# Joining the two parts of x into one product of 512 columns, and the two heads of a stick-breaking pair

## The chip, the cores and the metric

The kernel runs on one core of one Trainium2 chip. The metric is the device time of one execution in microseconds (us), taken from the first to the last instruction on the chip; lower is better. Several executions are measured and their median is compared.

## The reference, cut to what matters

A sequence of 256 tokens of width 1024 goes through two blocks, each of two layers, all in float32:

```
# first block, per layer
proj  = h @ w_in                      # 2048 columns: pool mixer, q, k, v
y_sb  = stick_breaking_attention(q, k, v)     # 8 heads of 64
h     = layer_norm(alpha*h + concat(pool_mixer(u), y_sb) @ w_out)
f     = (silu(h @ wg) * (h @ wu)) @ wd        # layer 0: one network of width 2816
                                              # layer 1: 8 experts of it, 2 per token
h     = layer_norm(alpha*h + f)
# stick-breaking attention, s < t only
A[t,s] = sigmoid(z_ts) * prod_{s<j<t} (1 - sigmoid(z_tj)),  z = q k^T / 8
# second block, per layer
z = rms_norm(x) @ w_in                # HGRN2 (q, f, i, g), 3 groups of dilated attention, 2 gates
x = x + (sigmoid(za)*(o_hg @ w_a) + sigmoid(zb)*(o_att @ w_b)) @ w_out
x = x + square(relu(rms_norm(x) @ w_up)) @ w_down      # width 4096
```

## The kernel before, in words

**Numbers in two parts.** Every large product is made of three matmuls of reduced-precision floats (fp32r). A weight tile `raw` is split into `whi` (ScalarE, L164) and `wlo` = raw - whi (VectorE, L166); activations are split into `xh` and `xl` likewise. `mm3` (L214 to L225) issues whi·xh, whi·xl and wlo·xh into the same PSUM columns.

**Weights.** `list_weights` writes out the order of all weight units, each 128 x 2048 floats (1 MB). `take` (L193) hands the next unit to the products: before it does, it emits the split of the unit two further on (`N_SPLIT` = 3, the present one counted), ScalarE first, then VectorE, and the DMA of a unit some eight ahead. Raw, whi and wlo tiles share 13 slots of the pool `wts`. The order of instructions on each engine is the order in which the program emits them; no scheduler moves them.

**Feature chunks.** `chunk_feat` (L273) makes 512 features for all 256 tokens, features on partitions: weights stationary, x moving with 256 columns. A chunk takes two weight units (j = 0, 1, the halves of the contraction); in each it goes over four blocks c of 128 features, and for each block over four contraction tiles with one `mm3` each, so 96 matmuls a chunk. The four blocks fill two PSUM banks of the pool `acc` (four banks), two blocks to a bank. There are 44 such chunks: 2 in each of the two stick-breaking mixers (q and k), 10 in the feed-forward network of layer 0 (`ffn`, L684), and in each layer of the second block (`second`, L1070) 2 for HGRN2, 6 for q and k of the dilated attention and 7 in the up part. `chunk_tok` (L252) is the sister with tokens on partitions and 512 moving columns; `down` (L290) is the product after the feed-forward or up part, with 512 moving columns.

**Side work.** Attention, pool mixing and the like are generators in the list `side`; `pump` advances the first two of them by one step. `chunk_feat` pumps after its second and fourth block, four times a chunk. Side work uses the PSUM pools `ms` and `tr` (two banks each). `down` drains what is left.

**What follows a chunk.** In `ffn` (L700 to L706): one Silu over the two gate blocks (ScalarE), one product with the two up blocks (VectorE), the high part (ScalarE), the low part (VectorE), all 512 wide. In the up part (L1171 to L1177), twice a chunk: Relu (ScalarE), product (VectorE), high part (ScalarE), low part (VectorE), 512 wide. For q and k of the dilated attention (L1118): two copies by ScalarE. The first chunk of both parts comes from `boundary` with tokens on partitions; the generator `first` evaluates it in one step and, in the next, transposes it into `tr` banks and splits it.

**Stick pair.** `stick_pair` (L606) is the side work for two heads, one after the other, each in a bank of its own (`ms`, then `tr`): scores, then Relu, VectorE, Exp, Ln, VectorE, then, two pumps later, the suffix sums by matmul and the last Exp. A pair takes five steps.

Of the kernel before, what the change touches and what calls it, by code (L numbers as in the profile page):

```python
# [10 lines left out]
F32 = mybir.dt.float32  # L11
F32R = mybir.dt.float32r
# [9 lines left out]
P = 128  # L22
T = 256
# [72 lines left out]
class Net:  # L96
# [176 lines left out]
    def chunk_feat(self, x):  # L273

        xh, xl = x
        out = [self.bank(), self.bank()]
        for j in range(2):
            w = self.take(1)[0]
            for c in range(4):
                o = out[c // 2][:, (c % 2) * T:(c % 2 + 1) * T]  # L280
                for k in range(4):
                    kt = 4 * j + k
                    self.mm3(o, xh[:, kt, :], xl[:, kt, :], w[0][:, k, c * P:(c + 1) * P],
                             w[1][:, k, c * P:(c + 1) * P], kt == 0 and c % 2 == 0, kt == 7,
                             w_stationary=True, skip_group_check=True)
                if c % 2 == 1:
                    self.pump()
        return out
# [137 lines left out]
    def run(self, stop=None):  # L426
# [4 lines left out]
        self.x = (self.main.tile([P, KT, T], F32R, name="xh"), self.main.tile([P, KT, T], F32R, name="xl"))  # L431
# [132 lines left out]
    def mixer(self, l, ps):  # L564
# [3 lines left out]
        with self.mixs:  # L568
# [12 lines left out]
            for j in range(2):  # L581
                ps = self.chunk_feat(self.x)
                nc.scalar.activation(q[:, 2 * j:2 * j + 2].rearrange("p c t -> p (c t)"), ps[0], AF.Identity,
                                     scale=0.125)
                nc.vector.tensor_copy(k[:, 2 * j:2 * j + 2].rearrange("p c t -> p (c t)"), ps[1])
                for c in (2 * j, 2 * j + 1):
                    self.side.append(self.stick_pair(c, q, k, pairs, work))
# [18 lines left out]
    def stick_pair(self, c, q, k, pairs, work):  # L606
        nc = self.nc
        mm = nc.tensor.matmul
        pairs[c] = []
        for hp in range(2):  # L610
            rows = slice(64 * hp, 64 * hp + 64)
            z = self.tr.tile([P, 512], F32, name="tr") if hp else self.ms.tile([P, 512], F32, name="ms")
            mm(z[:, 0:256], k[rows, c, 0:P], q[rows, c, :], start=True, stop=False, skip_group_check=True)
            mm(z[:, 256:384], k[rows, c, P:T], q[rows, c, P:T], start=False, stop=False, skip_group_check=True)
            for o in (0, 256):
                mm(z[:, o:o + P], self.identb, self.below, start=False, stop=False, skip_group_check=True)
            e = work.tile([P, 384], F32, name="e")
            pos = work.tile([P, 384], F32, name="pos")
            nc.scalar.activation(pos, z[:, 0:384], AF.Relu)
            nc.vector.scalar_tensor_tensor(e, pos, -2.0, z[:, 0:384], op0=OP.mult, op1=OP.add)  # L620
            nc.scalar.activation(e, e, AF.Exp)
            nc.scalar.activation(e, e, AF.Ln, bias=1.0)
            nc.vector.tensor_add(e, e, pos)
            yield
            yield
# [10 lines left out]
            pairs[c].append(att)  # L636
# [45 lines left out]
    def ffn(self, ps):  # L682
        nc, a, tc = self.nc, self.a, self.tc
        with tc.tile_pool(name="ffn", bufs=1) as pool, tc.tile_pool(name="ffnw", bufs=2) as work:  # L684
# [13 lines left out]
            self.side.append(first())  # L698
            for j in range(1, FF // 256):
                ps2 = self.chunk_feat(self.x)  # L700
                s = work.tile([P, 512], F32, name="s")
                nc.scalar.activation(s, ps2[0], AF.Silu)
                nc.vector.tensor_mul(s, s, ps2[1])
                h, l = (m[:, 2 * j:2 * j + 2].rearrange("p c t -> p (c t)") for m in hid)
                nc.scalar.activation(h, s, AF.Identity)
                nc.vector.tensor_sub(l, s, h.bitcast(F32))  # L706
                if j == 6:
                    g, b = self.load_rows((a["ln2_g"][0], a["ln2_b"][0]))
# [133 lines left out]
    def experts(self, gate, rank, xt, rest, iota1, sums, end):  # L842
        nc, a, tc = self.nc, self.a, self.tc
        mm = nc.tensor.matmul
        with tc.tile_pool(name="moew", bufs=2) as work:
# [4 lines left out]
            def gather(p):  # L850
# [7 lines left out]
                for i in range(2):  # L858
                    for k in range(0, KT, 2):
# [8 lines left out]
                        nc.scalar.activation(xg[i][:, k:k + 2].rearrange("p k s -> p (k s)"), ps, AF.Identity)  # L868
# [202 lines left out]
    def second(self, l, ps, stop=None):  # L1071
        nc, a, tc = self.nc, self.a, self.tc
        self.n_ahead = N_AHEAD - 1
        with tc.tile_pool(name="z", bufs=1) as pool, tc.tile_pool(name="zw", bufs=2) as work:
# [12 lines left out]
            ps = self.chunk_feat(self.x)  # L1087
            for i in range(2):
                c = slice(512 * i, 512 * i + 512)
                nc.scalar.activation(f[:, c], ps[i], AF.Sigmoid)  # L1090
                nc.scalar.activation(k[:, c], ps[i], AF.Sigmoid, scale=-1.0)
            for h in range(4):
                c = slice(T * h, T * h + T)
                nc.vector.tensor_scalar(f[:, c], f[:, c], lb[:, 4 + h:5 + h], lb[:, h:h + 1], op0=OP.mult, op1=OP.add)
                nc.vector.tensor_scalar(k[:, c], k[:, c], lb[:, 4 + h:5 + h], None, op0=OP.mult)
            ps = self.chunk_feat(self.x)
            for i in range(2):
                c = slice(512 * i, 512 * i + 512)
                nc.scalar.activation(q[:, c], ps[i], AF.Sigmoid)
                nc.vector.tensor_mul(q[:, c], q[:, c], ps[i])  # L1100
            og = pool.tile([P, 2, 512], F32, name="og")
# [8 lines left out]
            for g in range(3):  # L1110
                qk = []
                for i in range(2):
                    ps = self.chunk_feat(self.x)
                    if i == 1:
                        self.rotate(*qk[0], rope)
                    x = pool.tile([P, 4, T], F32, name="qa" if i == 0 else "ka", bufs=2)
                    for j in range(2):
                        nc.scalar.activation(x[:, 2 * j:2 * j + 2].rearrange("p c t -> p (c t)"), ps[j], AF.Identity)  # L1118
# [35 lines left out]
        with tc.tile_pool(name="up", bufs=1) as pool, tc.tile_pool(name="upw", bufs=2) as work:  # L1154
# [13 lines left out]
            self.side.append(first())  # L1168
            for j in range(1, FF2 // 512):
                ps2 = self.chunk_feat(self.x)  # L1170
                for i in range(2):  # L1171
                    s = work.tile([P, 512], F32, name="s")
                    nc.scalar.activation(s, ps2[i], AF.Relu)
                    nc.vector.tensor_mul(s, s, ps2[i])
                    h, lo = (m[:, 4 * j + 2 * i:4 * j + 2 * i + 2].rearrange("p c t -> p (c t)") for m in hid)
                    nc.scalar.activation(h, s, AF.Identity)
                    nc.vector.tensor_sub(lo, s, h.bitcast(F32))  # L1177
# [218 lines left out]
```

## Time and profile before

| what | value |
|---|---|
| median of 3 runs | 2150.21 us (2146.05 to 2150.62) |
| the profiled execution's own time | 2147.67 us |
| its span, first to last instruction | 2145.9 us |
| granted TensorE clock, mean | 0.991 of full speed |
| TensorE (PE) busy | 2097.9 us, 98% |
| VectorE (DVE) busy | 1497.7 us, 70% |
| ScalarE (ACT) busy | 1217.4 us, 57% |
| HBM read | 504.77 MB |

How to read it: PE is a matmul, PEld a weight load, L12 a line of the kernel. A matmul's duration is its latency: matmuls overlap, so the distance between the starts of two neighbours, not the duration, is what one costs in a stream. Queues of ACT and DVE are worked off in order. In what follows W stands for the ScalarE instruction of L164 (the high part of a weight unit) and w for the VectorE instruction of L166 (its low part).

### The profile page before, as it was taken

How to read it: one execution, taken by the hardware profiler on the slowest of the kernel's cores; microseconds unless marked ns; L12 is line 12 of the kernel's file. 1: busy time of each engine (PE TensorE's matmuls, PEld its weight loads, DVE VectorE, ACT ScalarE, POOL GpSimd, SP SyncE). 2: the span in 40 equal slices, each digit the busy share in tenths (PEclk: the TensorE clock that was granted, in tenths of full speed). 3: DMA queues.
4: the chain of work that ended last, by engine and by line, in shares of the span. 5: the costliest groups of instructions: out<-in, count | busy, mean ns of one | idle time of the engine just before them, and what ended most of it. 6: DMA issues, size and time to landing. Idle time of an engine off the chain costs nothing. (4 is left out here: it accounts for less than half of the span.)

```text
span 2145.9 us, 28621 instructions
## 1 busy us (share of the span) xinstructions
PE 2097.9 (98%) x11787; PEld 1823.0 (85%) x11787; DVE 1497.7 (70%) x1326; ACT 1217.4 (57%) x1199; POOL 81.0 (4%) x91
## 2 busy tenths in 40 slices
PE   7999999999999999999999799999999999999998
PEld 6889988788888888888888699988998899988987
DVE  6465464698888989898989566666655566666643
ACT  4544445677777777777777444464543434454542
POOL 1000000000000000000000101100000011100000
PEclk9999999999999999999999899999999999999999
DMA  9275555599999999999998454444754654436551
GB/s 319 79 224 188 190 163 216 192 357 367 364 339 368 368 348 361 373 350 348 367 357 305 142 182 140 144 159 138 235 191 144 222 164 155 136 130 221 191 194 62
DMA packets 240122, 509.33 MB, mean 237 GB/s; under 512 B 9360, under 2 KB 56592, under 8 KB 239984
## 3 DMA queue, kind: packets, MB, share of 16 engines
q1 hardware_dynamic: 236448, 496.21, 66.7%
q0 software_dynamic: 3248, 10.69, 1.6%
q8 instruction: 95, 1.56, 0.3%
q10 hardware_dynamic: 288, 0.52, 0.1%
q14 instruction: 43, 0.35, 0.0%
HBM read 504.77 MB, written 1.05 MB: 236 GB/s over the span
## 5 line engine op out<-in xcount | busy, mean ns | idle before, releaser
L166 DVE TENSOR_TENSOR wlo<-raw,whi 128x2048 fp32r<-128x2048 f32 x463 | 1062.1, 2296 | 356.9 <-ACT whi L164 308.0
L164 ACT ACTIVATE whi<-raw 128x2048 fp32r<-128x2048 f32 x467 | 887.0, 1915 | 259.2 <-PE acc L224 81.3
L223 PE MATMUL acc<-whi,xh 128*128 128x512 f32 x1168 | 469.1, 402 | 4.1 <-ACT xh L348 2.1
L224 PE MATMUL acc<-wlo,xh 128*128 128x512 f32 x1168 | 458.3, 392 | 2.3 <-DVE wlo L161 1.7
L225 PE MATMUL acc<-whi,xl 128*128 128x512 f32 x1168 | 459.9, 394 | 0.5 <-DVE xl L349 0.5
L219 PE MATMUL acc<-xh,whi 128*128 128x256 f32 x1408 | 404.8, 287 | 0.0
L221 PE MATMUL acc<-xh,wlo 128*128 128x256 f32 x1408 | 399.1, 283 | 0.0
L220 PE MATMUL acc<-xl,whi 128*128 128x256 f32 x1408 | 399.1, 283 | 0.0
L223 PE MATMUL acc<-whi,hidh 128*128 128x512 f32 x696 | 273.0, 392 | 0.0
L224 PE MATMUL acc<-wlo,hidh 128*128 128x512 f32 x696 | 271.6, 390 | 0.0
L219 PEld LDWEIGHTS acc<-xh,whi 128*128 128x128 f32 x1408 | 270.4, 192 | 1.3
L225 PE MATMUL acc<-whi,hidl 128*128 128x512 f32 x696 | 271.4, 390 | 0.0
L220 PEld LDWEIGHTS acc<-xl,whi 128*128 128x128 f32 x1408 | 270.5, 192 | 0.7
L221 PEld LDWEIGHTS acc<-xh,wlo 128*128 128x128 f32 x1408 | 270.3, 192 | 0.0
L225 PEld LDWEIGHTS acc<-whi,xl 128*128 128x128 f32 x1168 | 220.7, 189 | 52.6 <-DVE xl L349 5.9
L223 PEld LDWEIGHTS acc<-whi,xh 128*128 128x128 f32 x1168 | 221.2, 189 | 50.5 <-ACT xh L348 5.5
L224 PEld LDWEIGHTS acc<-wlo,xh 128*128 128x128 f32 x1168 | 221.3, 190 | 46.5 <-DVE wlo L161 2.3
L225 PEld LDWEIGHTS acc<-whi,hidl 128*128 128x128 f32 x696 | 130.8, 188 | 27.4
L223 PEld LDWEIGHTS acc<-whi,hidh 128*128 128x128 f32 x696 | 130.9, 188 | 25.9
L224 PEld LDWEIGHTS acc<-wlo,hidh 128*128 128x128 f32 x696 | 130.9, 188 | 25.7
L348 ACT ACTIVATE xh<-tr 128x512 fp32r<-128x512 f32 x40 | 22.5, 596 | 73.1 <-PE tr L355 72.8
L926 ACT ACTIVATE hidh<-tr 128x512 fp32r<-128x512 f32 (+1 forms) x48 | 27.0, 563 | 64.6 <-PE tr L355 64.6
(304 smaller groups left out, 1598.2 us busy)
## 6 DMA issues: line engine op xcount, KB each, us to landing
raw<-in_moe_wd_dram SPq DMA_DIRECT2D x88, 1024.0 KB, 6.7
raw<-in_moe_wg_dram SPq DMA_DIRECT2D x80, 1024.0 KB, 6.4
raw<-in_moe_wu_dram SPq DMA_DIRECT2D x80, 1024.0 KB, 6.3
raw<-in_w_in_dram SPq DMA_DIRECT2D x74, 1024.0 KB, 5.4
raw<-in_w_up_dram SPq DMA_DIRECT2D x32, 1024.0 KB, 5.4
raw<-in_w_down_dram SPq DMA_DIRECT2D x32, 1024.0 KB, 5.0
raw<-in_w_out_dram SPq DMA_DIRECT2D x16, 1024.0 KB, 5.0
raw<-in_ffn_wg_dram SPq DMA_DIRECT2D x22, 512.0 KB, 4.1
```

The source lines that it names most:

```text
L164: self.nc.scalar.activation(hi, raw, AF.Identity)
L166: self.nc.vector.tensor_sub(lo, raw, hi.bitcast(F32))
L219: mm(out, wh, xh, start=start, stop=False, **kw)
L220: mm(out, wh, xl, start=False, stop=False, **kw)
L221: mm(out, wl, xh, start=False, stop=stop, **kw)
L223: mm(out, xh, wh, start=start, stop=False, **kw)
L224: mm(out, xh, wl, start=False, stop=False, **kw)
L225: mm(out, xl, wh, start=False, stop=stop, **kw)
L348: self.nc.scalar.activation(h, v, AF.Identity)
L926: nc.scalar.activation(h[:, :n], v, AF.Identity)
```

## The change

`xh` and `xl` become the two halves of one tile `xx` (contraction tile, part, token), so one matmul moves both: whi·(xh, xl) with 512 columns into a whole bank, then wlo·xh with 256 columns into the bank's second half. A block now needs a bank of its own, and its two halves have to be added. `chunk_feat` no longer returns banks: it calls `sink(c, halves)` as soon as block c is complete, and each sink copies the first half (ScalarE) and adds the second (VectorE). Without `pools` the four banks come from `acc`; in the feed-forward and up parts blocks 0 and 1 take `acc` banks, block 2 a `tr` bank, block 3 an `ms` bank. `first` is advanced by its first step ahead of the chunks. `stick_pair` issues the scores of both heads together, with Abs, Exp, Ln and one VectorE instruction in place of Relu, VectorE, Exp, Ln, VectorE; a pair still takes five steps.

```diff
-    def chunk_feat(self, x):
+    def chunk_feat(self, sink, pools=None):
...
             for c in range(4):
-                o = out[c // 2][:, (c % 2) * T:(c % 2 + 1) * T]
+                if j == 0:
+                    out.append((pools or (self.acc,) * 4)[c].tile([P, 512], F32, ...))
                 for k in range(4):
                     kt = 4 * j + k
-                    self.mm3(o, xh[:, kt, :], xl[:, kt, :], w[0][:, k, c * P:(c + 1) * P], ...)
+                    mm(out[c], w[0][:, k, cw], self.xx[:, kt].rearrange("p i t -> p (i t)"), start=kt == 0, ...)
+                    mm(out[c][:, T:], w[1][:, k, cw], self.xx[:, kt, 0], start=False, stop=kt == 7, ...)
+                if j == 1:
+                    sink(c, (out[c][:, :T], out[c][:, T:]))
                 if c % 2 == 1:
                     self.pump()
...
     def stick_pair(self, c, q, k, pairs, work):
+        zs = [self.ms.tile([P, 512], F32, name="ms"), self.tr.tile([P, 512], F32, name="tr")]
+        for z, rows in zip(zs, heads):
             mm(z[:, 0:256], k[rows, c, 0:P], q[rows, c, :], start=True, stop=False, skip_group_check=True)
+        for z, rows in zip(zs, heads):
             mm(z[:, 256:384], k[rows, c, P:T], q[rows, c, P:T], start=False, stop=False, skip_group_check=True)
...
+            nc.scalar.activation(e, z[:, 0:384], AF.Abs)
+            nc.scalar.activation(e, e, AF.Exp, scale=-1.0)
             nc.scalar.activation(e, e, AF.Ln, bias=1.0)
-            nc.vector.tensor_add(e, e, pos)
+            nc.vector.scalar_tensor_tensor(e, z[:, 0:384], 0.0, e, op0=OP.max, op1=OP.add)
...
     def ffn(self, ps):
-            self.side.append(first())
+            f = first()
+            next(f)
+            self.side.append(f)
             for j in range(1, FF // 256):
-                ps2 = self.chunk_feat(self.x)
...
+                def sink(c, ps, j=j, gs=gs, us=us):
+                    s = us[:, c - 2] if c > 1 else gs[:, c]
+                    nc.scalar.activation(s, ps[0], AF.Identity)
+                    nc.vector.tensor_add(s, s, ps[1])
+                    if c < 2:
+                        nc.scalar.activation(s, s, AF.Silu)
+                    else:
+                        h, l = (m[:, 2 * j + c - 2] for m in hid)
+                        nc.vector.tensor_mul(s, s, gs[:, c - 2])
+                        nc.scalar.activation(h, s, AF.Identity)
+                        nc.vector.tensor_sub(l, s, h.bitcast(F32))
+
+                self.chunk_feat(sink, (self.acc, self.acc, self.tr, self.ms))
...
     def second(self, l, ps, stop=None):
+            def joined(dst, ps):
+                nc.scalar.activation(dst, ps[0], AF.Identity)
+                nc.vector.tensor_add(dst, dst, ps[1])
...
+                    def sink(c, ps, i=i, x=x):
+                        if i == 1 and c == 3:
+                            self.rotate(*qk[0], rope)
+                        joined(x[:, c], ps)
...
             for j in range(1, FF2 // 512):
-                ps2 = self.chunk_feat(self.x)
...
+                def sink(c, ps, j=j):
+                    v = work.tile([P, T], F32, name="s2")
+                    joined(v, ps)
+                    nc.vector.scalar_tensor_tensor(v, v, 0.0, v, op0=OP.max, op1=OP.mult)
+                    h, lo = (m[:, 4 * j + c] for m in hid)
+                    nc.scalar.activation(h, v, AF.Identity)
+                    nc.vector.tensor_sub(lo, v, h.bitcast(F32))
+
+                self.chunk_feat(sink, (self.acc, self.acc, self.tr, self.ms))
```

In the two HGRN2 chunks the sink joins the halves and then applies Sigmoid (twice for the forget gate) block by block. In the mixers the sinks of q and k are one ScalarE and one VectorE instruction a block. The gather of the expert layer writes its copy of x through the strided `xx`.

## Rows read from the trace of the kernel before

**Rows 1.** The page, part 1: busy us, share and instructions.
```profile
PE 2097.9 (98%) x11787; PEld 1823.0 (85%) x11787; DVE 1497.7 (70%) x1326; ACT 1217.4 (57%) x1199; POOL 81.0 (4%) x91
```
**Rows 2.** PE's waits over the span: us in total, times, longest.
```profile
PE tr L355 <- DVE r L423: 14.0, 2, 12.1
PE tr L355 <- ACT whi L160: 11.6, 1, 11.6
```
**Rows 3.** The page, part 5: feature chunk's first matmul (busy us, mean ns).
```profile
L219 PE MATMUL acc<-xh,whi 128*128 128x256 f32 x1408 | 404.8, 287 | 0.0
```
**Rows 4.** Timeline of PE in an up chunk: start us, us; ten matmuls.
```profile
2007.81 0.28 PE L219 MATMUL acc<-xh,whi 128*128 128x256 f32 x1
...
2008.89 0.28 PE L219 MATMUL acc<-xh,whi 128*128 128x256 f32 x1
```
**Rows 5.** Timeline of PE in the down part; seven matmuls.
```profile
2079.73 0.39 PE L225 MATMUL acc<-whi,hidl 128*128 128x512 f32 x1
...
2081.09 0.39 PE L225 MATMUL acc<-whi,hidl 128*128 128x512 f32 x1
```
**Rows 6.** Busy time of one up chunk: us, PE, PEld, DVE, ACT, POOL.
```profile
2005.54:2017.06 11.52, 11.52 (x99) 11.52 (x98) 7.26 (x7) 6.17 (x6) 0.00 (x0) 1.00 0.62 187
```
**Rows 7.** Timeline of ACT in the up part.
```profile
2006.90 0.63 ACT L1176 ACTIVATE hidh<-s 128x512 fp32r<-128x512 f32 x1 [0.76 <-DVE s L1174]
2007.44 1.90 ACT L164 ACTIVATE whi<-raw 128x2048 fp32r<-128x2048 f32 x1
2011.25 1.91 ACT L164 ACTIVATE whi<-raw 128x2048 fp32r<-128x2048 f32 x1 [1.91 <-PE acc L221]
```
**Rows 8.** Timeline of DVE in the same stretch.
```profile
2007.57 0.69 DVE L1177 TENSOR_TENSOR hidl<-s,hidh 128x512 fp32r<-128x512 f32 x1 [0.70 <-ACT hidh L1176]
2009.37 2.29 DVE L166 TENSOR_TENSOR wlo<-raw,whi 128x2048 fp32r<-128x2048 f32 x1 [1.11 <-ACT whi L164]
2013.20 2.29 DVE L166 TENSOR_TENSOR wlo<-raw,whi 128x2048 fp32r<-128x2048 f32 x1 [1.53 <-ACT whi L164]
2015.41 0.68 DVE L1174 TENSOR_TENSOR s<-s,acc 128x512 f32<-128x512 f32 x1
```
**Rows 9.** Groups by form, 256 columns wide: busy us, mean ns.
```profile
L651 ACT ACTIVATE mixh<-ms 128x256 fp32r<-128x256 f32 x8 | 3.1, 384 | 9.6 <-PE ms L649 9.6
L1354 DVE TENSOR_TENSOR oa<-oa,ms 128x256 f32<-128x256 f32 x8 | 3.4, 421 | 8.4 <-PE ms L1348 8.0
L1353 DVE TENSOR_TENSOR oa<-oa,w 128x256 f32<-128x256 f32 x8 | 3.3, 414 | 0.0
```
**Rows 10.** Timeline of DVE, an instruction that reads its predecessor's result.
```profile
1317.30 0.69 DVE L1321 TENSOR_REDUCE w<-ms 128x2 f32<-128x512 f32 x1
1318.02 0.17 DVE L1322 TENSOR_SCALAR w<-w 128x2 f32<-128x2 f32 x1
```
**Rows 11.** Timeline of DVE and ACT in the feed-forward part.
```profile
155.48 2.29 DVE L166 TENSOR_TENSOR wlo<-raw,whi 128x2048 fp32r<-128x2048 f32 x1 [1.11 <-ACT whi L164]
157.81 1.92 ACT L164 ACTIVATE whi<-raw 128x2048 fp32r<-128x2048 f32 x1 [2.36 <-DVE wlo L166]
203.95 1.91 ACT L164 ACTIVATE whi<-raw 128x2048 fp32r<-128x2048 f32 x1 [2.41 <-PE acc L220]
```
**Rows 12.** Timeline: the split of `first` in the up part, ACT and DVE.
```profile
1976.31 1.08 ACT L348 ACTIVATE hidh<-tr 128x512 fp32r<-128x512 f32 x2 [5.46 <-PE tr L355]
1976.94 1.29 DVE L349 TENSOR_TENSOR hidl<-tr,hidh 128x512 fp32r<-128x512 f32 x2 [2.75 <-ACT hidh L348]
```
**Rows 13.** Timeline of PE: one head's scores in a stick pair.
```profile
359.63 0.70 PE L613 MATMUL ms<-q,k 64*128 64x256 f32 x2
360.17 0.38 PE L614 MATMUL ms<-q,k 64*128 64x128 f32 x2
```
**Rows 14.** Timeline in the dilated attention: a w, and the evictions of a q chunk.
```profile
1322.40 2.29 DVE L166 TENSOR_TENSOR wlo<-raw,whi 128x2048 fp32r<-128x2048 f32 x1 [1.29 <-ACT whi L164]
1325.99 1.08 ACT L1118 ACTIVATE qa<-acc 128x512 f32<-128x512 f32 x2
```

More of the change, by code (lines that the diff above doesn't have):

```diff
@@ L271, in chunk_tok @@
         return out
-    def chunk_feat(self, x):
-        xh, xl = x
-        out = [self.bank(), self.bank()]
+    def chunk_feat(self, sink, pools=None):
+        mm = self.nc.tensor.matmul
+        out = []
         for j in range(2):
@@ L581, in mixer @@
             for j in range(2):
[L582 to L585, printed above, removed]
+                def sink(c, ps, j=j):
+                    if c < 2:
+                        d = q[:, 2 * j + c]
+                        nc.scalar.activation(d, ps[0], AF.Identity, scale=0.125)
+                        nc.vector.scalar_tensor_tensor(d, ps[1], 0.125, d, op0=OP.mult, op1=OP.add)
+                    else:
+                        d = k[:, 2 * j + c - 2]
+                        nc.scalar.activation(d, ps[0], AF.Identity)
+                        nc.vector.tensor_add(d, d, ps[1])
+                self.chunk_feat(sink)
                 for c in (2 * j, 2 * j + 1):
@@ L608, in stick_pair @@
         mm = nc.tensor.matmul
[L609 to L612, printed above, removed]
+        heads = (slice(0, 64), slice(64, P))
+        zs = [self.ms.tile([P, 512], F32, name="ms"), self.tr.tile([P, 512], F32, name="tr")]
+        for z, rows in zip(zs, heads):
             mm(z[:, 0:256], k[rows, c, 0:P], q[rows, c, :], start=True, stop=False, skip_group_check=True)
+        for z, rows in zip(zs, heads):
             mm(z[:, 256:384], k[rows, c, P:T], q[rows, c, P:T], start=False, stop=False, skip_group_check=True)
+        for z in zs:
             for o in (0, 256):
                 mm(z[:, o:o + P], self.identb, self.below, start=False, stop=False, skip_group_check=True)
[L617 to L621, printed above, removed]
+        es = []
+        for z in zs:
+            e = work.tile([P, 384], F32, name="e", bufs=4)
+            nc.scalar.activation(e, z[:, 0:384], AF.Abs)
+            nc.scalar.activation(e, e, AF.Exp, scale=-1.0)
             nc.scalar.activation(e, e, AF.Ln, bias=1.0)
-            nc.vector.tensor_add(e, e, pos)
+            nc.vector.scalar_tensor_tensor(e, z[:, 0:384], 0.0, e, op0=OP.max, op1=OP.add)
+            es.append(e)
             yield
-            yield
+        yield
+        for hp, (z, e) in enumerate(zip(zs, es)):
             mm(z[:, 0:256], self.suffix, e[:, 0:256], start=False, stop=False, skip_group_check=True)
@@ L635, in stick_pair @@
             nc.scalar.activation(att, z[:, 0:384], AF.Exp)
-            pairs[c].append(att)
+            pairs.setdefault(c, []).append(att)
+            if hp == 0:
+                yield
     def stick_values(self, v, pairs, mix):
@@ L1112, in second @@
                 for i in range(2):
-                    ps = self.chunk_feat(self.x)
-                    if i == 1:
-                        self.rotate(*qk[0], rope)
                     x = pool.tile([P, 4, T], F32, name="qa" if i == 0 else "ka", bufs=2)
-                    for j in range(2):
-                        nc.scalar.activation(x[:, 2 * j:2 * j + 2].rearrange("p c t -> p (c t)"), ps[j], AF.Identity)
+                    def sink(c, ps, i=i, x=x):
+                        if i == 1 and c == 3:
+                            self.rotate(*qk[0], rope)
+                        joined(x[:, c], ps)
+                    self.chunk_feat(sink)
                     rot = pool.tile([32, 4, T], F32, name="rot")
@@ L1166, in first, with sink @@
                     self.split_to(hid, self.transpose4(hs[t]), 0, t)
-            self.side.append(first())
+            f = first()
+            next(f)
+            self.side.append(f)
             for j in range(1, FF2 // 512):
-                ps2 = self.chunk_feat(self.x)
[L1171 to L1177, printed above, removed]
+                def sink(c, ps, j=j):
+                    v = work.tile([P, T], F32, name="s2")
[5 more added lines that the diff above has]
+                self.chunk_feat(sink, (self.acc, self.acc, self.tr, self.ms))
             acc3 = self.down(hid, FF2 // P)
```

50 lines of the change are left out of this document (26 added, 24 removed).

## The prediction

> **What bounds the kernel now.** I read the page first: PE is busy for 98% of the span, DVE for 70% [rows 1]. A busy matmul need not be a matmul at its peak, so I went on to PE's waits: the two longest, 14.0 and 11.6 us, lie where a layer begins or the kernel starts [rows 2] and have nothing to do with the chunks. Inside the feature chunks PE waits for nobody. What one matmul costs there is read from the timeline and not from its duration of 287 ns [rows 3], which is latency: nine distances in a chunk make 1.08 us, so a matmul of 256 columns costs 120.0 ns [rows 4]; six distances of the down part make 1.36 us, so one of 512 columns costs 226.7 ns [rows 5]. The difference, 106.7 ns for 256 columns, leaves 13.3 ns that every matmul costs whatever its width. A chunk of 96 matmuls takes 11.52 us of PE, and in that time DVE is busy for 7.26 and ACT for 6.17 us [rows 6]. So the bound is the number and width of the matmuls, and two helpers stand behind it with some room.
>
> **What the joint product gives.** Three matmuls of 256 columns (360.0 ns) become one of 512 and one of 256: 226.7 + 120.0 = 346.7 ns. The weights are loaded behind the neighbouring matmul in both streams [rows 4, 5], so I take the loads as hidden in the mixture too. A chunk falls from 11.52 to 11.09 us; 44 chunks with 32 such groups save 1408 x 13.3 ns = 18.7 us: 1.7 in the mixers, 4.3 in the feed-forward part, 6.8 in HGRN2 and attention, 6.0 in the up parts. The bounds are 18.7 us and nothing.
>
> **What the sinks cost in the up part.** This decides. Before, a chunk's results leave by two chains 512 wide; now four chains 256 wide go back and forth between ACT and DVE, both strictly in program order, and the splits of later weights are queued behind them. Prices at 256 columns: ACT 0.38 out of PSUM [rows 9], 0.41 from SBUF (an estimate: at 512 columns two out of PSUM take 1.08 together [rows 14], one from SBUF 0.63 [rows 7], a few hundredths more apiece); DVE 0.42 with PSUM, 0.41 without [rows 9]. An instruction that reads its predecessor's result starts 0.03 us after its end, on the same engine [rows 10] or the other [rows 7, 8]; one that doesn't starts about 0.08 before it (w to the next: 2.21 us for a duration of 2.29 [rows 8]).
>
> One sink on DVE: add 0.42 + 0.03, square of Relu 0.41 + 0.03, then the wait for ACT's high part 0.41 + 0.04, then the low part, after which the next add starts 0.34 later: 1.68 us. The next copy by ACT runs beside the low part. From the first add to the end of the fourth high part: 3 x 1.68 + 1.30 = 6.34 us. Only then comes the next unit's W, in program order: its w starts 1.84 us after the end of the high part (from 2007.53 to 2009.37) [rows 7, 8]. That w and the next block DVE for 4.42 us before the next chunk's first add. **The helpers' period is 6.34 + 1.84 + 4.42 = 12.60 us, and PE's is 11.09.** They fall 1.51 us behind with every chunk. (Before, with two sinks, the same sum is below 10 us against 11.52.)
>
> How long does that stay hidden? Take 0 as the start of the second unit of the first chunk. Its W starts there, when PE gives a slot free [rows 7], its w ends at 4.24, the first add starts at 4.16, the fourth high part ends at 10.50, and the w behind it ends at 10.50 + 1.84 + 2.29 = 14.63. PE wants that unit at the start of the third chunk, 5.55 + 11.09 = 16.64: 2.01 us to spare. After six more periods the margin is 2.01 - 6 x 1.51 - 0.2 = -7.3 us (0.2: the down part's units are a little shorter than a chunk's, 5.44 us). So PE waits at the weight units from the fourth or fifth chunk on, 7.3 us a layer, **14.5 us in two layers**, against 6.0 gained there. Later, in the down part, DVE has one w in 5.44 us and catches up. The bounds: nothing, if the helpers keep pace, and 20 us, if every instruction costs 0.1 us more than I take.
>
> **The feed-forward part.** The gate sinks are ACT, DVE, ACT: 0.42 + 0.03 + 0.32 + 0.38 + 0.03 = 1.18 us each; the two up sinks 1.68 and 1.30. Period: 1.18 x 2 + 1.68 + 1.30 + 1.84 + 4.42 = 11.60 us. The margin at first is 16.64 - (4.16 + 5.34 + 1.84 + 2.29) = 3.0 us; over ten chunks it becomes 3.0 - 9 x 0.51 - 0.2 = -1.8. That is the lower bound. In the first chunks, though, W starts 0.04 us after the end of the w before it, which the trace names as its releaser, later PE [rows 11]; if W there really waits for that w, the two don't overlap, and the period is 5.34 + 8.33 = 13.67 us for six chunks: 10 us lost. PE's own release falls at the same moment in this trace, so the row can't tell them apart; I take the middle, **6.0 us**.
>
> **Smaller terms.** The third block of the first chunk now goes into a `tr` bank just after `first` has transposed into both of them. The split that frees a bank takes 1.08 us on ACT and 1.29 on DVE for two banks, DVE starting 0.63 after ACT [rows 12], so one bank is free some 1.3 us after its transposes, of which the second four transposes hide a part: 1.0 us at each of three places, **3.0 us** (0 to 4). In HGRN2 and attention one block's add must be done 4.16 us (12 groups) after the block, before the next chunk needs the bank. In one dilated chunk the w ahead of the adds ends at 1324.7 and the chunk at about 1325.4 [rows 14], so the first add, then at 1325.0, has half a microsecond to spare; the added rotation ahead of the fourth add costs more. I take **2.0 us** for 12 chunks (0 to 6). In the mixers a sink is one instruction on each engine, and DVE is half idle: nothing, as PE's 24 matmuls of a half chunk cover it; without that cover four adds, 1.7 us a chunk. The stick pair keeps its five steps and loses one DVE instruction a head; the engines aren't the bound there. The strided gather copies as many elements as before: nothing. The scores of the two heads lie in different halves of the partitions, and one head's take 0.54 us for 256 columns [rows 13], about 0.81 with the narrower ones (an estimate). No row shows two heads side by side; bounds 0 and 8 x 0.81 = 6.5 us gained, and by the one row there is, where the parts of one head run one after the other, I take **-1.0**.
>
> The Trainium skill (TensorE: Matmul & The Clock Gate, Part 3, The mechanism) says that matmuls on different row groups run concurrently. By it the stick pairs would give near the 6.5 us and the sum would be some 5 us lower; no run here shows it.
>
> **Sum:** -18.7 - 1.0 + 14.5 + 6.0 + 3.0 + 2.0 = +5.8 us on the profiled execution's 2147.67 us. That execution stands 2.5 us below the median of the runs; on the median it makes 2150.2 + 5.8 = 2156 us. About 0.2% (4.3 us) is what a measurement of this kernel can tell from no change.
>
> **The rivals.**
> 1. *Faster: the helpers keep pace.* The place is the up sink; it decides at 1.30 us (11.09 less 6.26, over four, with its shorter last part, gives 1.30) in place of my 1.68. For it: DVE's busy time in a chunk would be 4.6 + 4 x 1.25 = 9.6 us, below 11.09, and PE has never waited for a w so far. Against it: program order, and the 0.70 us that DVE waits for ACT in every sink already [rows 8]. Then -18.7 - 1.0 + 3.0 makes 2133 us.
> 2. *No change.* The up part falls behind as worked out, but W in the feed-forward part depends on PE alone and attention hides its adds: -18.7 - 1.0 + 14.5 + 1.8 + 2.0 = -1.4, 2149 us. For it: the late row of [rows 11].
> 3. *The joint product doesn't give what it says.* The 13.3 ns go with the columns or the loads and not with the matmul, so the group still takes 360 ns. For it: no row shows 512 and 256 columns in turn. Against it: the two streams' distances fit one constant. Helpers then have 11.52 us: the margin in the up part is 2.6 - 6 x 1.08 - 0.2 = -4.1 us a layer, and the sum is 8.2 + 2.5 + 3.0 + 1.0 = +14.7, 2165 us. The Trainium skill (TensorE: Matmul & The Clock Gate, Back-to-back issue gap) speaks for this side: it puts the fixed part of a warm matmul at 2.5 ns, by which one matmul less in 1408 groups saves 3.5 us only. The trace disagrees, with 13.3 ns [rows 4, 5].
>
> **How the numbers follow.** My forecast has 0.40 (most likely between 2150 and 2166), the first rival 0.27, the second 0.25, the third 0.08. Slower by over 0.2%: 0.08 and five sixths of the forecast's share, 0.42. Faster: the first rival and some of the second, 0.31. The rest, 0.27, is within 0.2%. The range from 2132 to 2166 us takes in the first rival's value, the third's, and the bounds of the sinks; 2 in 10 are left outside.
>
> **What would show it.** Right: starts of the 512- and 256-column matmuls 226.7 and 120.0 ns apart; in PE's waits a new row for wlo L166 in the feed-forward and up parts, of some 6 and 14 us; the distance of two chunks 11.09 us at first, 12.6 later; DVE at over 80% in the up part with the sub waiting for ACT in every sink; PE waiting once at a `tr` bank in the first chunk of each part. Wrong: no wait of PE for a wlo, which is the first rival; groups that take 360 ns, which is the third; long waits of PE for the adds of attention, which I price at 2 us.

## The result, and the profile after

The changed kernel takes 2162.21 us (median of 5 runs, 2157.37 to 2162.71), the kernel before 2150.05 us beside it: ratio 1.0052, 95% interval 1.0041 to 1.0063. It is 12.2 us slower; the prediction said 5.8. Its profiled execution took 2162.71 us, with a span of 2160.9 us.

The page of the kernel after, part 1 (busy us, share, instructions):

```profile
PE 2086.7 (97%) x10379; PEld 1740.9 (81%) x10379; DVE 1566.6 (72%) x1562; ACT 1251.4 (58%) x1379; POOL 82.1 (4%) x91
```

PE issues 1408 matmuls fewer and is busy for 11 us less than in [rows 1], while the span is 15 us longer. So PE waits more. (Some 2 of the 15 us lie ahead of the chunks: the profiled execution of the kernel before starts its first chunk at 33.1 us, the kernel after and every kernel of the experiments, those with the old product too, at 35.0 to 36.3.) PE's waits after (us in total, times, longest):

```profile
PE tr L362 <- DVE r L430: 14.8, 2, 12.7
PE tr L362 <- DVE h L416: 11.5, 4, 10.5
PE acc L290 <- DVE wlo L166: 10.0, 9, 1.3
PE acc L224 <- DVE wlo L166: 5.7, 6, 1.3
PE tr L288 <- DVE hidl L356: 5.2, 3, 1.7
...
PE tr L362 <- DVE y L1336: 1.6, 2, 0.8
```

The first two were there before [rows 2]. The next two are PE at a weight unit whose w is late (L290: in a chunk; L224: elsewhere, mostly in the down part). Of their 15.7 us 14.4 lie in the two up parts with what follows them, 0.6 in the feed-forward part, and 0.6 behind the second mixer, where the kernel before waits as long. The fifth is the third block of the first chunk at the bank into which `first` has just transposed, 1.7 us at each of three places. The last is in attention: a transpose waits for DVE. Why w is late stands in the timeline of DVE in an up chunk after (start us, duration, [idle before <- releaser]); the line numbers are those of the new kernel: L1121 copy, L1122 add, L1217 square of Relu, L1219 and L1220 high and low part.

```profile
2016.00 0.41 DVE L1122 TENSOR_TENSOR s<-s,acc 128x256 f32<-128x256 f32 x1
2016.45 0.42 DVE L1217 SCALAR_TENSOR_TENSOR s<-s 128x256 f32<-128x256 f32 x1
2017.36 0.42 DVE L1220 TENSOR_TENSOR hidl<-s,hidh 128x256 fp32r<-128x256 f32 x1 [0.48 <-ACT hidh L1219]
2017.70 0.41 DVE L1122 TENSOR_TENSOR s<-s,acc 128x256 f32<-128x256 f32 x1
...
2022.46 0.42 DVE L1220 TENSOR_TENSOR hidl<-s,hidh 128x256 fp32r<-128x256 f32 x1 [0.48 <-ACT hidh L1219]
2024.26 4.49 DVE L166 TENSOR_TENSOR wlo<-raw,whi 128x2048 fp32r<-128x2048 f32 x2 [1.38 <-ACT whi L164]
2028.68 0.41 DVE L1122 TENSOR_TENSOR s<-s,acc 128x256 f32<-128x256 f32 x1
```

From add to add a sink takes 1.70 us, and from one chunk's first add to the next 12.68 us: the two engines hand each block back and forth, W waits for the fourth high part, and w for W. The busy share doesn't show this. In such a chunk (stretch; PE, PEld, DVE, ACT, POOL; clock, DMA share, GB/s) DVE is busy for 9.22 of 12.68 us, 73%:

```profile
2016.30:2028.98 12.68, 11.57 (x67) 9.83 (x66) 9.22 (x15) 6.36 (x10) 0.00 (x0) 1.00 0.52 167
```

The second surprise is PE's own rate in chunks without a wait. Timeline of PE in the feed-forward part after, 32 pairs apart:

```profile
163.46 0.40 PE L288 MATMUL acc<-xx,whi 128*128 128x512 f32 x1
163.70 0.28 PE L290 MATMUL acc<-xx,wlo 128*128 128x256 f32 x1
163.81 0.40 PE L288 MATMUL acc<-xx,whi 128*128 128x512 f32 x1
...
174.77 0.40 PE L288 MATMUL acc<-xx,whi 128*128 128x512 f32 x1
```

163.46 to 174.77 is 11.31 us, 353.4 ns a pair and not 346.7. Half of the joint product's gain is missing here.

### The profile page after: what moved, and what is told of

Same layout as the page of the kernel before. It is cut to its first block, busy times and chain, and to the rows that moved or that the text cites. A ratio compares the mean times of both kernels' runs of the same rounds, so it can differ in the third digit from the quotient of the medians.

```text
span 2160.9 us, 26263 instructions
## 1 busy us (share of the span) xinstructions
PE 2086.7 (97%) x10379; PEld 1740.9 (81%) x10379; DVE 1566.6 (72%) x1562; ACT 1251.4 (58%) x1379; POOL 82.1 (4%) x91
## 5 line engine op out<-in xcount | busy, mean ns | idle before, releaser
L223 PE MATMUL acc<-whi,xx 128*128 128x512 f32 x1168 | 468.4, 401 | 6.6 <-ACT whi L160 4.6
L225 PE MATMUL acc<-whi,xx 128*128 128x512 f32 x1168 | 459.1, 393 | 0.5 <-DVE xx L356 0.5
L224 PE MATMUL acc<-wlo,xx 128*128 128x512 f32 x1168 | 457.2, 391 | 2.1 <-DVE wlo L161 1.5
L288 PE MATMUL acc<-xx,whi 128*128 128x512 f32 x1024 | 370.0, 402 | 0.0
L290 PE MATMUL acc<-xx,wlo 128*128 128x256 f32 x1024 | 287.9, 281 | 10.0 <-DVE wlo L166 10.0
L224 PE MATMUL acc<-wlo,hidh 128*128 128x512 f32 x696 | 272.0, 391 | 5.1 <-DVE wlo L166 5.1
L223 PEld LDWEIGHTS acc<-whi,xx 128*128 128x128 f32 x1168 | 220.8, 189 | 53.3 <-ACT whi L160 5.5
L225 PEld LDWEIGHTS acc<-whi,xx 128*128 128x128 f32 x1168 | 220.2, 189 | 52.8 <-DVE xx L356 5.9
L224 PEld LDWEIGHTS acc<-wlo,xx 128*128 128x128 f32 x1168 | 220.9, 189 | 46.4 <-DVE wlo L161 2.1
L288 PEld LDWEIGHTS acc<-xx,whi 128*128 128x128 f32 x1024 | 192.4, 188 | 44.4
L290 PEld LDWEIGHTS acc<-xx,wlo 128*128 128x128 f32 x1024 | 193.4, 189 | 14.0 <-DVE wlo L166 13.2
L224 PEld LDWEIGHTS acc<-wlo,hidh 128*128 128x128 f32 x696 | 130.8, 188 | 32.9 <-DVE wlo L166 7.3
L1219 ACT ACTIVATE hidh<-s 128x256 fp32r<-128x256 f32 x56 | 23.4, 418 | 92.3 <-DVE s L1217 92.3
L288 PE MATMUL tr<-xx,whi 128*128 128x512 f32 x192 | 70.1, 399 | 5.2 <-DVE hidl L356 5.2
L288 PE MATMUL ms<-xx,whi 128*128 128x512 f32 x192 | 69.8, 397 | 0.0
```

Source lines behind the costliest of these rows:

```text
L223: mm(out, xh, wh, start=start, stop=False, **kw)
L224: mm(out, xh, wl, start=False, stop=False, **kw)
L225: mm(out, xl, wh, start=False, stop=stop, **kw)
L288: mm(out[c], w[0][:, k, cw], self.xx[:, kt].rearrange("p i t -> p (i t)"), start=kt == 0, stop=False, skip_group_check=True)
L290: mm(out[c][:, T:], w[1][:, k, cw], self.xx[:, kt, 0], start=False, stop=kt == 7, skip_group_check=True)
L1219: nc.scalar.activation(h, v, AF.Identity)
```

## The experiments

Each was timed in five rounds or more beside the kernel before on its own chip; ratios and differences are against that (its medians lay between 2148.89 and 2150.03 us). An interval reaches 2 to 3.5 us to either side; smaller steps are read from traces, one for each kernel.

**1. The stick pair alone.** The kernel before, with the new `stick_pair` and nothing else; the diff of that function stands with the change.

> The kernel before with the new stick pair and nothing else. Theory (the two heads' score matmuls run side by side, as the trace after shows them starting 7 ns apart, so that a pair costs 0.85 us less, eight pairs): about 7 us less than before, 2143 us (2142 to 2145). Rival (the prediction's term: one head's scores follow the other's): 1 us less, 2149 us. A second rival (the two extra steps at which a pair gives way delay the later chunks): nothing or slower.

2141.58 us, ratio 0.9956 (0.9942 to 0.9969): 8.5 us less. In the trace 4.0 us go in the first mixer and 4.4 between the second mixer's chunks and attention; every other chunk keeps its distance. The timeline of PE in this kernel shows how:

```profile
54.07 0.48 PE L613 MATMUL ms<-q,k 64*128 64x256 f32 x1
54.08 0.48 PE L613 MATMUL tr<-q,k 64*128 64x256 f32 x1
54.39 0.38 PE L613 MATMUL ms<-q,k 64*128 64x256 f32 x1
54.40 0.38 PE L613 MATMUL tr<-q,k 64*128 64x256 f32 x1
...
54.92 0.28 PE L618 MATMUL ms<-bm 128*128 128x128 bf16 x2
55.13 0.37 PE L219 MATMUL acc<-xh,whi 128*128 128x256 f32 x1
```

The two heads' products start 0.01 us apart; after 1.06 us both have their scores and masks.

**2. The same pair, its products in turn.**

```diff
         for z, rows in zip(zs, heads):
             mm(z[:, 0:256], k[rows, c, 0:P], q[rows, c, :], ...)
-        for z, rows in zip(zs, heads):
             mm(z[:, 256:384], k[rows, c, P:T], q[rows, c, P:T], ...)
-        for z in zs:
             for o in (0, 256):
                 mm(z[:, o:o + P], self.identb, self.below, ...)
```

> The kernel before with the new stick pair (2141.6 us), but with the score products of one head and its mask all ahead of those of the other, as the kernel before has them; ACT and DVE as in the new pair. Theory (the 8.5 us are the two heads' products side by side): about 7 us of the gain go, 2148 to 2150 us. Rival (they come from the elementwise chain, one instruction of DVE less for a head and both heads in flight): 2142 us, as with the products in turn.

2149.31 us, ratio 0.9999 (0.9988 to 1.0009): the whole gain is gone. Its timeline:

```profile
54.33 0.70 PE L613 MATMUL ms<-q,k 64*128 64x256 f32 x2
54.86 0.38 PE L614 MATMUL ms<-q,k 64*128 64x128 f32 x2
55.17 0.28 PE L616 MATMUL ms<-bm 128*128 128x128 bf16 x2
55.39 0.70 PE L613 MATMUL tr<-q,k 64*128 64x256 f32 x2
...
56.24 0.29 PE L616 MATMUL tr<-bm 128*128 128x128 bf16 x2
56.33 0.37 PE L219 MATMUL acc<-xh,whi 128*128 128x256 f32 x1
```

54.33 to 56.33 is 2.00 us against 1.06: 0.94 us a pair, 7.5 us for eight. Two heads on different halves of the partitions run side by side. The Trainium skill (TensorE: Matmul & The Clock Gate, Part 3, The mechanism) says that matmuls on different row groups overlap, and the trace agrees, with starts 0.01 us apart. The shorter elementwise chain gives nothing that the medians can tell, and at most 0.8 us in the traces.

**3. The up part undone.** Its products, banks and sinks as before.

```diff
-                self.chunk_feat(sink, (self.acc, self.acc, self.tr, self.ms))
+                ps2 = self.chunk_feat_old(self.x)
+                for i in range(2):
+                    nc.scalar.activation(s, ps2[i], AF.Relu)
...
```

> The kernel after with the up part as before: three products of 256 columns, two banks, sinks 512 wide. Theory (the up parts lost 9.3 and 9.4 us and nothing later depends on them): 18.7 us less than after, 2143 to 2145 us, and PE waits for no wlo. Rival (the loss sits in the first chunk's banks and in what precedes the up part, and the waits only move): 2152 us or more.

2142.67 us, ratio 0.9960 (0.9946 to 0.9974). Against before that is 7.4 us less, where the kernel after was 12.2 more: the two up parts cost 19.6 us. That the loss is there was right; its causes were not yet told apart.

**4. The first chunk's third block in another bank.** One bank in three chunks changes, nothing else.

```diff
-                self.chunk_feat(sink, (self.acc, self.acc, self.tr, self.ms))
+                self.chunk_feat(sink, (self.acc, self.acc, self.ms if j == 1 else self.tr, self.ms))
```

> The kernel after with the third block of the first chunk of the feed-forward part and of the two up parts in an ms bank, so that it no longer waits for the transposes' split. Theory (the wait of 1.7 us at three places adds to whatever follows, since the helpers' first sink and split also start from PE): 5.2 us less than after, 2157 us. Rival (in the up parts the helpers' chain sets the time, so PE only waits as much longer at the weights): only the feed-forward part's 1.7 us, 2160.5 us.

2151.10 us, ratio 1.0005 (0.9996 to 1.0014): 11 us less than after, twice what the three waits amount to. Both theories fell. PE's timeline in this kernel gives a part of the reason, again 32 pairs apart in the feed-forward part:

```profile
161.08 0.39 PE L288 MATMUL acc<-xx,whi 128*128 128x512 f32 x1
161.31 0.28 PE L290 MATMUL acc<-xx,wlo 128*128 128x256 f32 x1
161.43 0.39 PE L288 MATMUL acc<-xx,whi 128*128 128x512 f32 x1
...
172.17 0.39 PE L288 MATMUL acc<-xx,whi 128*128 128x512 f32 x1
```

11.09 us: 346.6 ns a pair, as predicted. The stream has two rates, 347 and 353 ns, and keeps the one that it has until something interrupts it. In both kernels the first chunk of the feed-forward part begins at 353, and the transposes of `first` interrupt it after the second block. Here the stream goes on at 347 and keeps that for the nine chunks behind; in the kernel after, with the wait at the `tr` bank, it goes on at 353. Where PE waits for a w, the rate changes too, in either direction. Why the stream has two rates isn't shown. Neither the granted clock nor the DMA goes with the rate, as two chunks of the kernel after and then two of this kernel show (stretch; PE, PEld, DVE, ACT, POOL; clock, DMA share, GB/s):

```profile
163.46:174.77 11.31, 11.31 (x66) 9.81 (x65) 7.70 (x10) 6.04 (x10) 0.00 (x0) 1.00 0.32 104
139.79:151.09 11.30, 11.30 (x66) 9.81 (x65) 6.84 (x9) 5.79 (x8) 0.00 (x0) 1.00 0.79 247
161.08:172.17 11.09, 11.09 (x66) 9.79 (x65) 7.16 (x10) 6.37 (x10) 0.00 (x0) 1.00 0.53 171
138.89:149.99 11.10, 11.10 (x67) 9.80 (x66) 7.56 (x10) 6.00 (x10) 0.00 (x0) 1.00 0.83 262
```

In the traces the feed-forward part gains 3.4 us and each up part 4.0. Each of the three first chunks is 2.1 us shorter (in the feed-forward part 11.58 in place of 13.68 us), and a chunk behind at the other rate 0.21 us. That is the whole gain in the feed-forward part, and 2.6 of the 4.0 us in an up part. The other 1.4 us lie with the helpers. In the kernel after, DVE's second w in the second chunk waits for PE; here it follows the first at once (DVE, the kernel after, then this one):

```profile
2001.12 2.29 DVE L166 TENSOR_TENSOR wlo<-raw,whi 128x2048 fp32r<-128x2048 f32 x1 [2.31 <-PE ms L288]
...
1987.33 4.68 DVE L166 TENSOR_TENSOR wlo<-raw,whi 128x2048 fp32r<-128x2048 f32 x2 [1.38 <-ACT whi L164]
```

Why that w waits for PE only in the kernel after isn't shown.

**5. The products in another order.** For each block and half four wide ones, then four narrow ones.

```diff
                 for k in range(4):
                     mm(out[c], w[0][:, k, cw], self.xx[:, kt]..., ...)
+                for k in range(4):
                     mm(out[c][:, T:], w[1][:, k, cw], self.xx[:, kt, 0], ...)
```

> The kernel after with another order of the products of a block and half: the four of 512 columns first, then the four of 256. Theory (a change from 256 to 512 columns and back costs the 6.7 ns by which a pair takes 353.4 and not 346.7 ns; in a row each width costs its own 226.7 and 120.0 ns): three changes of four go, a chunk takes 32 x 348.4 ns = 11.15 us, 0.16 us less in the 30 chunks that wait for no helper, 5 us in all: 2157 us; the up parts gain nothing, as their helpers set the pace. Rival (the 6.7 ns belong to the pair of widths, whatever the order; or to the weight load ahead of the wide product): a chunk stays at 11.30 us and the time at 2162 us.

2159.48 us, ratio 1.0045 (1.0031 to 1.0059). PE's timeline in the feed-forward part:

```profile
151.96 1.09 PE L288 MATMUL acc<-xx,whi 128*128 128x512 f32 x4
152.89 0.63 PE L292 MATMUL acc<-xx,wlo 128*128 128x256 f32 x4
...
163.19 1.09 PE L288 MATMUL acc<-xx,whi 128*128 128x512 f32 x4
```

A chunk takes 11.23 us, 350.9 ns a pair, between the two rates; within a run of four the wide ones stand 234 ns apart, not 226.7. So the extra time isn't the change of width alone, and both accounts fell.

**6. The feed-forward part undone**, in the same way:

```diff
-                self.chunk_feat(sink, (self.acc, self.acc, self.tr, self.ms))
+                ps2 = self.chunk_feat_old(self.x)
+                nc.scalar.activation(s, ps2[0], AF.Silu)
...
```

> The kernel after with the feed-forward part as before. Theory (from the two traces: its first chunk costs 1.7 us more, nine chunks gain 0.21 us each, the down part behind it costs 1.2 us more): 1.7 us less than after, 2160.5 us. Rival (the prediction's middle: W tied to w, 6 us of waits against 4.3 gained and 1 for the bank): 2.7 us less, 2159.5 us; with the upper bound 6.7 us less. No difference at all would say that what the joint product gains there pays for the rest.

2158.02 us, ratio 1.0036 (1.0023 to 1.0049), 8.4 us over before. From the first mixer's last chunk to the second mixer's first it needs 265.88 us, the kernel after 267.57: 1.7 us less, as the first account had it. The rest of the difference lies behind that part and within the interval.

**7. Three tries at the helpers' order.** First the low part one block later, so that DVE can add the next block while ACT makes the high part:

```diff
                     nc.scalar.activation(h, v, AF.Identity)
-                    nc.vector.tensor_sub(lo, v, h.bitcast(F32))
+                    last.append(lambda: nc.vector.tensor_sub(lo, v, h.bitcast(F32)))
+                    for low in (last[c - 1:c] if c < 3 else last[2:]):
+                        low()
```

> The kernel after with the low part of each block of the up part one block later, so that DVE adds and squares the next block while ACT makes the high part. Same instructions, other order. Theory (DVE's wait of 0.48 us for ACT's high part in every sink makes the helpers' period 12.67 us): the period becomes 3 x 1.26 + 1.30 + 1.84 + 4.42 = 11.34 us, nearly PE's 11.31; PE's 15.7 us of waits for wlo go, and with them most of the 18.7 us that the two up parts lost: 2144 to 2149 us. Rival (it is DVE's or ACT's amount of work, or the bank that a sink gives back late): the period stays above 12.4 us, and the time at 2160 to 2163 us.

2160.96 us, ratio 1.0044 (1.0030 to 1.0057): nothing gained that the medians can tell (2.5 us in the traces), and nothing decided, since a sink took up to 1.75 us and the period stayed at 12.70. The tile of a block comes from two slots, so ACT's next copy waited for the low part just moved back. Then with four slots:

```diff
-                    v = work.tile([P, T], F32, name="s2")
+                    v = vs[c // 2][:, c % 2]
```

> The order of the run before this one with four slots for a chunk's blocks in place of two (the first try kept two, and there ACT's next copy waited for the low part that had just been moved back: the sink took 1.74 us, 0.04 more than in the kernel after). Theory (the helpers' wait for each other makes the period): a sink takes 1.26 us on DVE, the period is 3 x 1.26 + 1.30 + 1.84 + 4.42 = 11.34 us against PE's 11.30, the 15.7 us of waits for wlo in the up parts go: 2145 to 2149 us. Rival (DVE's and ACT's amount of work, or banks given back late): the period stays above 12.4 us and the time above 2158 us.

2158.47 us, ratio 1.0042 (1.0029 to 1.0055). The sink takes 1.63 us now and the period is 12.49 us (the 12.68 of the next expectation is the kernel after's); the timelines of ACT and DVE in this kernel (L1121 is the copy, L1122 the add, L1219 the square, L1221 the high part) show what is late next:

```profile
2027.79 0.42 ACT L1221 ACTIVATE hidh<-s 128x256 fp32r<-128x256 f32 x1 [0.94 <-DVE s L1219]
2028.12 0.36 ACT L1121 ACTIVATE s<-tr 128x256 f32<-128x256 f32 x1
...
2028.51 0.42 DVE L1122 TENSOR_TENSOR s<-s,tr 128x256 f32<-128x256 f32 x1 [0.42 <-ACT s L1121]
```

DVE's add waits for ACT's copy, which stands behind the high part of the block before in ACT's order, which waits for DVE. The wait had only moved to the other engine. So the third try, on the kernel of experiment 4, keeps the four slots (`v(c)` is block c's) and has ACT copy the next block first:

```diff
+                    nc.scalar.activation(v(c), ps[0], AF.Identity)
+                    if c:
+                        high(c - 1)
+                    nc.vector.tensor_add(v(c), v(c), ps[1])
+                    nc.vector.scalar_tensor_tensor(v(c), v(c), 0.0, v(c), op0=OP.max, op1=OP.mult)
+                    if c:
+                        low(c - 1)
```

> The kernel with the third block's bank in ms (2151.1 us) and the up sinks with ACT's copy of the next block ahead of the high part of the last: in the two tries before, the copy still stood behind the high part in ACT's program order, so that DVE's add waited for it in every sink (1.64 us a sink, period still 12.68 us). Now neither engine waits for the other inside a chunk. Theory (the order of the two engines makes the period): a sink takes about 1.2 us on DVE, the period is 3 x 1.2 + 1.3 + 1.84 + 4.42 = 11.1 to 11.2 us against PE's 11.09, the 13.7 us of waits for wlo in the up parts go but for a microsecond or two: 2137 to 2141 us. Rival (the amount of DVE's work, or the splits of the weights by themselves, set the pace): the chunks stay at 12.68 us and the time at 2148 to 2151 us.

2134.16 us, ratio 0.9928 (0.9915 to 0.9941): 17 us less than experiment 4. Against that kernel the slots, the late low part and ACT's order change together; slots and low part had given some 3 us in the second try, so the rest is ACT's order. DVE does the same work in its timeline, without a gap in the sinks, 1.13 us from add to add between later blocks and 11.09 us from one chunk's first add to the next (L1224 is the add, L1225 the square):

```profile
2003.25 0.41 DVE L1224 TENSOR_TENSOR s<-s,acc 128x256 f32<-128x256 f32 x1
2003.69 0.42 DVE L1225 SCALAR_TENSOR_TENSOR s<-s 128x256 f32<-128x256 f32 x1
2004.04 0.42 DVE L1224 TENSOR_TENSOR s<-s,acc 128x256 f32<-128x256 f32 x1
...
2009.46 2.29 DVE L166 TENSOR_TENSOR wlo<-raw,whi 128x2048 fp32r<-128x2048 f32 x1 [1.38 <-ACT whi L164]
2012.13 2.29 DVE L166 TENSOR_TENSOR wlo<-raw,whi 128x2048 fp32r<-128x2048 f32 x1 [0.38 <-ACT whi L164]
2014.34 0.42 DVE L1224 TENSOR_TENSOR s<-s,acc 128x256 f32<-128x256 f32 x1
```

In that stretch DVE is busy for 82%:

```profile
2003.25:2014.34 11.09, 11.09 (x65) 9.78 (x64) 9.05 (x16) 6.60 (x10) 0.00 (x0) 1.00 0.56 194
```

Of PE's waits for w (first experiment 4, then this kernel) little is left:

```profile
PE acc L290 <- DVE wlo L166: 7.8, 8, 1.5
PE acc L224 <- DVE wlo L166: 5.9, 7, 1.3
...
PE acc L224 <- DVE wlo L166: 1.1, 2, 0.6
...
PE acc L290 <- DVE wlo L166: 0.4, 1, 0.4
```

The order of two engines, not the amount of their work, had set the pace.

**8. Two combinations.** The second try of 7 with the bank of 4 and the order of 5:

> The kernel after with the three edits together: the up sinks one block behind with four slots, the first chunk's third block in an ms bank, and the products ordered four wide, four narrow. Theory: 15.7 us (waits for wlo) + 5.2 us (bank) + 3 us (351 in place of 353.4 ns in 44 chunks of 32 groups) less than after: 2138 us, below the kernel before and below the kernel before with the new stick pair alone (2141.6 us). Rival (each edit only moves the wait to the next late thing): 2145 us or more.

2146.47 us, ratio 0.9987 (0.9978 to 0.9995). It missed 2138: its helpers still waited for each other (a sink 1.63 us, the period 12.48). It is faster than before by a little. Then experiment 7's third kernel with the feed-forward sinks in the same order:

```diff
+                    nc.scalar.activation(v(c), ps[0], AF.Identity)
+                    if c:
+                        high(c - 1)
+                    nc.vector.tensor_add(v(c), v(c), ps[1])
+                    if c > 1:
+                        nc.vector.tensor_mul(v(c), v(c), gs[:, c - 2])
```

> The run before this one with the same order in the feed-forward part, too (ACT's copy of the next block ahead of Silu or the high part of the last). Theory: the period there falls from 11.63 us below PE's 11.09, the wait that appears in the ninth chunk (0.7 us) and about a microsecond in the down part behind it go: 1 to 2 us less than the run before. Rival (the feed-forward part's helpers are not what its down part waits for): the same time.

2132.74 us, ratio 0.9917 (0.9901 to 0.9932). The two intervals overlap; in the traces the feed-forward part falls by 2.5 us more, and all its chunks keep 346.7 ns.

**9. HGRN2 and attention as before**, on that kernel:

```diff
-                    self.chunk_feat(sink)
+                    ps = self.chunk_feat_old(self.x)
...
+                    for j in range(2):
+                        nc.scalar.activation(x[:, 2 * j:2 * j + 2]..., ps[j], AF.Identity)
```

> The fastest kernel so far (2132.7 us) with HGRN2 and attention as before: products of 256 columns, sinks 512 wide. Theory (from the traces: there the 16 chunks gain some 4 us, and two side waits a layer, 0.8 and 0.7 us, of PE for work that the new adds hold up, and the slower phase of the product in the chunks of f and q, take that back): no difference, 2132 to 2133.5 us. Rival (the prediction's terms: 6.8 us gained, 2.0 lost): 4.8 us slower, 2137.5 us.

2130.63 us, ratio 0.9918 (0.9905 to 0.9932): no difference. In the traces the stretch from the first of these chunks to the up part takes 282.47 and 282.49 us, with the joint product 283.28 and 282.83. Nothing is gained there; in every trace with the joint product in the kernel after's order the HGRN2 chunks run at 353 ns a pair. Both kernels beat the one before by 17 to 18 us, and are the fastest here.

## Why the prediction was right and wrong

The sign and the main mechanism were right. The sum is half of what was measured, and it comes that near by luck: large terms of both signs were mis-sized and cancel in part.

- **The up part's helpers** (+14.5): right in kind and close in size. The period was forecast at 12.60 us and is 12.68, a sink at 1.68 and 1.70; the first wait comes in the fourth chunk; PE's waits for w come to 14.4 us, and taking the cause away gave 17.0 (experiment 7). That 14.4 is so near is luck in part: PE ran at 11.30 us a chunk and not at 11.09, which left less to wait for, and the second chunk's w lost 2.3 us that no term foresaw. With the bank moved (experiment 4) the same waits come to 11.8 us. Only the sign named for it was wrong: DVE at over 80%. By the prediction's own figures it is 76% (9.6 of 12.60 us), measured 73%; it is above 80% where DVE no longer waits (experiment 7, 9.05 of 11.09 us). The first rival, 2133 us, decided "at 1.30 in place of 1.68", and experiment 7 went below that, to 1.13, by order and slots. That its time is the rival's is luck: the bank's wait is gone there, too, the pair gives 8.5 us and not 1.0, the joint product some 8 and not 18.7.
- **The joint product** (-18.7, bounds 18.7 and nothing): the failing step is that the pair's cost, 346.7 ns, holds in every chunk. It holds in part of the chunks, and there the gain is as forecast: in experiment 8's second kernel the feed-forward part is 4.2 us shorter than before and the up part of the first layer 2.9 us (forecast 4.3 and 3.0). At 353.4 ns, as in most chunks of the kernel after, it is half, which is half of the third rival. In HGRN2 and attention, priced at -6.8 with +2.0 for waits, it is about zero. PE waits there twice a layer, 0.8 and 0.7 us, for side work on DVE and ACT, not for the banks that I had priced; with the old products and sinks (experiment 9) both waits are gone. The mixers' 1.7 us don't show either: against experiment 1 the first mixer is 0.4 us shorter, and the stretch from the second one's chunks to HGRN2 lies between 0.8 us less and 1.1 more. The Trainium skill (TensorE: Matmul & The Clock Gate, Back-to-back issue gap) puts a warm matmul's fixed part at 2.5 ns; the trace agrees at neither rate, as one matmul fewer in a group saved 13.4 ns at the one and 6.6 at the other.
- **The stick pair** (-1.0, bounds 0 and 6.5): the step that failed took the row of one head in turn [rows 13] as the nearest for two heads side by side. The gain is 8.5 us, 2 us beyond the end given; the scores save 0.84 us a pair, near the estimate of 0.81, and the masks, which were left out, 0.1 (experiments 1 and 2).
- **The bank behind `first`** (+3.0): the wait is 1.7 us a place and not 1.0, and removing it gave 11 us, since it also leaves the stream behind it on the slower rate and goes with a later w in the up parts. Nothing in the trace of before could show the rates: there the stream has one, 360.0 ns.
- **The feed-forward part** (+6.0): W isn't tied to w. The period is 11.63 us in most chunks, the lower end (11.60), and PE ran at 11.30, not 11.09; so the wait for w came to 0.6 us. At 11.09 (experiment 4) it is 1.3, and setting the helpers in order gave 1.4 us by the medians, 2.5 in the trace, near that end's 1.8. The upper end, 10 us, isn't what its terms give: six chunks of 2.58 us less the margin of 3.0 make 12.5.

One rival is added up wrongly: the second counts 2.0 for attention, which its own condition rules out, and leaves out the bank's 3.0. By its terms it makes -0.4, 2150 us.

By the runs: stick pair -8.5, joint product -8.1 (by subtraction: what experiment 8's second kernel, 16.6 us below before, has beyond the pair), the helpers' order +17.0 and +1.4, the bank +11.1. That makes +12.9 us; measured is +12.2. The sum is no test of its own, since each term is a step between kernels on the way from before to after.

## What to carry to other kernels

When an evacuation is cut into smaller pieces that pass between two in-order engines, add up the round trip from program order and compare it with the producer's period; a busy share of 73% can hide that it is the bound. Issue the next piece's first step ahead of this piece's second one on both engines, and look at the slots of the tile that carries it: with only one or two of these in place, 1 to 3 us of 17 were gained by the medians. Price a wait not by its length only, but by what the stream does after it.

## What the hardware showed that was not expected

An alternating stream of 512- and 256-column matmuls ran at 346.7 or 353.4 ns a pair at the same granted clock of 1.00 (experiment 4). At the faster rate each pair takes 346 to 348 ns, at the slower three pairs in turn take some 349, 350 and 361. The rate changed where other matmuls or a wait for a weight interrupted the stream, and once, in experiment 4's kernel at 1532 us, at a new weight unit without a wait in the list. Wide ones in a row with x moving stood 234 ns apart, those of the down part 226.7 [rows 5]. The cause of either stays open. Matmuls of 64 rows on different halves of the partitions started 0.01 us apart: 0.94 us of 2.00 saved for a pair with its masks.
